# A batched matmul with x loaded ahead of its weights, all casts on VectorE, all PSUM copies on ScalarE, and one buffer of cast weights and of x_t

## The chip, the cores and the metric

The kernel runs on one core of a Trainium2 chip. The metric is the device time of one execution in microseconds (us), taken as the median of several executions. "Granted clock" is the TensorE clock that the profile records, as a share of full speed.

## The reference

```python
# x (8, 16, 256, 512) float32, weight (8, 16, 512, 384) float32
def reference(x, weight):
    return np.matmul(x, weight).astype(np.float32)      # 128 products of 256x512 by 512x384
```

## The kernel before

The 128 batches go in 32 groups of four. For each group the DMA loads x in one transfer (2.10 MB) and the weights in two (1.57 MB each), and the result leaves in one store (1.57 MB). The operands are cast to bf16, x is transposed by TensorE, and 128 matmuls of 128x384 make the result. Each engine has its own loop and waits on counting semaphores; `BIAS` is an offset that keeps the counts positive.

```python
    XS, WS, OS = 2, 2 * G // D, 4       # slots of x_sb, w_sb (half a group each), out_sb
    BS, TS, WBS = 1, 2, 2 * G           # buffers of x_bf, x_t, and of cast weights (per batch)
    PT, PO = 4, 2                       # PSUM buffers of transposes and of products
    LAG = 4                             # groups loaded ahead

    def load(e, t, U, s):               # SyncE: the two halves of w, then x
        n = t * U + s
        for d in range(G // D):
            ...
            e.wait_ge(w_cast, n * (G * S) + ((d + 1) * D * S - 2 * G * S))
            e.dma_start(w_sb[slot][:], ...).then_inc(w_in[slot], 16)
        ...
        e.wait_ge(x_cast, n * T + (1 - XS) * T)
        e.dma_start(x_sb[s % XS][:], ...).then_inc(x_in[s % XS], 16)

    def prepare(e, t, U, s):            # VectorE: casts of w, then copies of x_t
        n = t * U + s
        e.wait_ge(p_made, n * T + (BIAS - T))     # products of the group before last are done
        ...                                       # 8 casts of w_sb into w_bf
        for q in range(T):                        # T = 4
            e.wait_ge(t_made, n * T + (q + 1 + BIAS))
            e.tensor_copy(out=x_t[s % TS][:, 2 * q : 2 * q + 2], in_=pt[...][:].bitcast(bf16))

    def multiply(e, t, U, s):           # TensorE
        ...                             # 16 transposes (4 for each x_bf cast), then 128 matmuls
```

ScalarE casts x (`cast_x`) and copies the products out of PSUM (`copy_out`).

Of the kernel before, what the change touches and what calls it, by code (L numbers as in the profile page):

```python
# [9 lines left out]


@with_exitstack
def kernel(
# [6 lines left out]
    nc = tc.nc  # L20
    P = 128

    b1, b2, M, K = x.shape
# [4 lines left out]
    x_rows = x.rearrange("b1 b2 m k -> (b1 b2 m) k")  # L28
# [4 lines left out]
    bf16 = mybir.dt.bfloat16  # L33
# [6 lines left out]
    G = 4  # L40
    C = P // G
    R = G * M // P
    T = R // 2
# [3 lines left out]
    NG = B // G  # L47

    XS, WS, OS = 2, 2 * G // D, 4
    BS, TS, WBS = 1, 2, 2 * G  # L50
    PT, PO = 4, 2

    LAG = 4

    ctx.enter_context(tc.tile_critical(no_gpsimd_drain=True))  # L55

    def sbuf(name, shape, dtype, n):
        return [
            ctx.enter_context(nc.sbuf_tensor(f"{name}{s}", shape, dtype)) for s in range(n)
        ]  # L60

    def psum(name, shape, dtype, n):
        return [
            ctx.enter_context(nc.psum_tensor(f"{name}{s}", shape, dtype)) for s in range(n)
        ]

    def sems(name, n):
        return [tc.alloc_semaphore(f"{name}{s}") for s in range(n)]
# [3 lines left out]
    x_sb = sbuf("x_sb", [P, R, K], fp32, XS)  # L72

    x_bf = sbuf("x_bf", [P, R, S, HP, KO], bf16, BS)
    x_t = sbuf("x_t", [P, R, KO // 2, P, 2], bf16, TS)
# [3 lines left out]
    pt = psum("pt", [P, 2, KO // 2, P], fp32, PT)  # L79
# [5 lines left out]
    id_done, x_cast, w_cast, t_made, t_copied, p_made, o_copied = (  # L85
        sems(name, 1)[0]
        for name in (
            "id_done", "x_cast", "w_cast", "t_made", "t_copied", "p_made", "o_copied"
        )
    )  # L90
    x_in, w_in, o_out = sems("x_in", XS), sems("w_in", WS), sems("o_out", OS)


    BIAS = 8


    def load(e, t, U, s):
        n = t * U + s
        for d in range(G // D):
            slot = (s * (G // D) + d) % WS  # L100
            if not isinstance(n, int) or n >= 2:
                e.wait_ge(w_cast, n * (G * S) + ((d + 1) * D * S - 2 * G * S))
            e.dma_start(  # L103
                w_sb[slot][:],
                w_rows[bass.ds(n * (G * K) + d * (D * K), D * K)].rearrange(
                    "(p k) n -> p k n", k=S * KO
                ),
            ).then_inc(w_in[slot], 16)
        if not isinstance(n, int) or n >= XS:
            e.wait_ge(x_cast, n * T + (1 - XS) * T)  # L110
        e.dma_start(  # L111
            x_sb[s % XS][:],
            x_rows[bass.ds(n * (G * M), G * M)].rearrange("(p r) k -> p r k", r=R),
        ).then_inc(x_in[s % XS], 16)

    def store(e, t, U, s, pieces=1):
        n = t * U + s
        dram = o_rows[bass.ds(n * (G * M), G * M)].rearrange("(p r) n -> p r n", r=R)
        for q in range(pieces):
            rows = slice(q * R // pieces, (q + 1) * R // pieces)  # L120
            e.wait_ge(o_copied, n * T + ((q + 1) * T // pieces + BIAS))
            e.dma_start(out=dram[:, rows], in_=out_sb[s % OS][:, rows]).then_inc(
                o_out[s % OS], 16
            )

    def cast_x(e, t, U, s, q):
        n = t * U + s
        if q == 0:
            e.wait_ge(x_in[s % XS], (t * (U // XS) + s // XS) * 16 + 16)
        e.wait_ge(t_made, n * T + (q + 1 - T + BIAS))  # L130
        rows = slice(2 * q, 2 * q + 2)
        e.copy(  # L132
            out=x_bf[s % BS][:, rows],
            in_=x_sb[s % XS][:, rows].rearrange("p r (q s c) -> p r s q c", s=S, c=KO),
        ).then_inc(x_cast, 1)

    def prepare(e, t, U, s):
        n = t * U + s
        e.wait_ge(p_made, n * T + (BIAS - T))
        for d in range(G // D):  # L140
            slot = (s * (G // D) + d) % WS
            e.wait_ge(
                w_in[slot], (t * (U * G // D // WS) + s * G // D // WS) * 16 + 16
            )
            for a in range(D):
                for h in range(S):
                    e.tensor_copy(  # L147
                        out=w_bf[(s * G + d * D + a) % WBS][h * HP : (h + 1) * HP],
                        in_=w_sb[slot][a * HP : (a + 1) * HP, h * KO : (h + 1) * KO, :],
                    ).then_inc(w_cast, 1)  # L150
        for q in range(T):
            e.wait_ge(t_made, n * T + (q + 1 + BIAS))
            e.tensor_copy(  # L153
                out=x_t[s % TS][:, 2 * q : 2 * q + 2],
                in_=pt[(s * T + q) % PT][:].bitcast(bf16),
            ).then_inc(t_copied, 1)

    def multiply(e, t, U, s):
        n = t * U + s
        words = x_bf[s % BS][:].rearrange("p r s q c -> p r (s q c)").bitcast(fp32)  # L160
        for q in range(T):
            e.wait_ge(x_cast, n * T + (q + 1))
            e.wait_ge(t_copied, n * T + (q + 1 - PT + BIAS))
            for rr in range(2):
                for h in range(KO // 2):
                    ins = e.transpose(  # L166
                        pt[(s * T + q) % PT][:, rr, h, :],
                        words[:, 2 * q + rr, h :: KO // 2],
                        identity[:],
                    )  # L170
            ins.then_inc(t_made, 1)
        e.wait_ge(w_cast, n * (G * S) + G * S)
        for q in range(T):
            e.wait_ge(t_copied, n * T + (q + 1 + BIAS))
            e.wait_ge(o_copied, n * T + (q + 1 - PO + BIAS))
            for rr in range(2):
                for ko in range(KO):
                    for i in range(G):
                        mine = slice(i * C, (i + 1) * C)
                        ins = e.matmul(  # L180
                            po[(s * T + q) % PO][mine, rr, :N],
                            x_t[s % TS][:, 2 * q + rr, ko // 2, mine, ko % 2],
                            w_bf[(s * G + i) % WBS][:, ko, :],
                            start=(ko == 0),
                            stop=(ko == KO - 1),
                        )
            ins.then_inc(p_made, 1)

    def copy_out(e, t, U, s, q):
        n = t * U + s  # L190
        if q == 0:
            e.wait_ge(o_out[s % OS], (t * (U // OS) + s // OS) * 16 + 16)
        e.wait_ge(p_made, n * T + (q + 1 + BIAS))  # L193
        e.copy(  # L194
            out=out_sb[s % OS][:, 2 * q : 2 * q + 2, :],
            in_=po[(s * T + q) % PO][:, :, :N],
        ).then_inc(o_copied, 1)
# [7 lines left out]
    def on_sync(e):  # L205
        U = OS
        for n in range(LAG):
            load(e, 0, NG, n)
        rounds = (NG - LAG) // U
        with e.Fori(0, rounds) as t:  # L210
            for s in range(U):
                load(e, t, U, LAG + s)
                store(e, t, U, s)
        for n in range(rounds * U, NG):
            if n + LAG < NG:
                load(e, 0, NG, n + LAG)
            store(e, 0, NG, n, T if n == NG - 1 else 1)
        for s in range(OS):
            e.wait_ge(o_out[s], 16 + 16 * (NG // OS + (T - 1 if s == (NG - 1) % OS else 0)))

    def on_vector(e):
        U = 2
        e.sem_inc(t_copied, BIAS)
        with e.Fori(0, NG // U) as t:
            for s in range(U):
                prepare(e, t, U, s)

    def on_tensor(e):
        U = 2
        e.sem_inc(t_made, BIAS)  # L230
        e.sem_inc(p_made, BIAS)
        e.wait_ge(id_done, 2)

        pe = mybir.EngineType.PE
        with nc.Fori(0, NG // U, engines=OrderedEngineSet([pe]), head_slot={pe: 0}) as t:
            for s in range(U):
                multiply(e, t, U, s)

    def on_scalar(e):
        U = OS  # L240
        e.sem_inc(o_copied, BIAS)
        for s in range(OS):
            e.sem_inc(o_out[s], 16)

        with e.Fori(0, NG // U) as t:
            for s in range(U):
                for q in range(T):
                    cast_x(e, t, U, s, q)
                for q in range(T):
                    copy_out(e, t, U, s, q)  # L250

    on_gpsimd(nc.gpsimd)
    on_sync(nc.sync)
    on_vector(nc.vector)
    on_tensor(nc.tensor)
    on_scalar(nc.scalar)


# [28 lines left out]
```

## Time and profile before

| | before |
|---|---|
| time, median of 3 | 518.83 us (518.81 to 519.08) |
| span of the profiled execution | 517.2 us |
| mean granted clock | 0.803 |
| VectorE busy per group | 10.4 us |
| ScalarE busy per group | 7.4 us |
| DMA per group, at 429 GB/s | 15.9 us |

The prediction below shows the lines and the sums that these numbers come from. The profile is to be read in this order: the DMA row of the 40 slices (is the memory full?), the chain that ended last (what set the end?), and then the groups with what ended the idle time in front of them (which waits stand between the engines?). Here the DMA is full (90% or more in every slice but the first and the last) and the engines are not (VectorE 64%, TensorE 59%, ScalarE 46%).

### The profile page before, as it was taken

The numbers are of one execution on the slowest core, as the hardware profiler recorded it, in microseconds if no ns is written. First come the engines' busy times: TensorE is split into PE (matmuls) and PEld (weight loads), VectorE is DVE, ScalarE is ACT, GpSimd is POOL, SyncE is SP. The second block draws the span as 40 slices with busy tenths as digits, with TensorE's granted clock in tenths as the row PEclk, the third lists the DMA queues.
The fourth block names the chain that finished last, engine by engine and source line by source line (L and its number), as shares of the span: only waits on it lengthen the run. The fifth ranks groups of instructions, "written<-read, shape, count | busy, mean of one in ns | idle before, by whom it ended". The sixth has DMA issues, their size and how long they took to land.

```text
span 517.2 us, 11523 instructions
## 1 busy us (share of the span) xinstructions
PE 306.6 (59%) x4608; PEld 200.6 (39%) x4608; DVE 332.8 (64%) x384; ACT 236.7 (46%) x264; POOL 0.7 (0%) x6
## 2 busy tenths in 40 slices
PE   0478776556665457645577554776446765467752
PEld 0345444334443334433344332444324443244431
DVE  3698875667556676556675566855658656676550
ACT  0465564443644436435355354454444544544441
POOL 0000000000000000000000000000000000000000
PEclk9998877878777887878777778877788877778777
DMA  8999999999999999999999999999999999999996
GB/s 340 430 423 424 424 432 426 429 428 430 432 427 427 427 428 432 429 427 430 426 431 431 426 429 430 427 432 427 427 429 429 427 433 425 430 428 430 429 428 251
DMA packets 18869, 218.18 MB, mean 422 GB/s; under 512 B 2096, under 2 KB 2096, under 8 KB 2608
## 3 DMA queue, kind: packets, MB, share of 16 engines
q1 hardware_dynamic: 18864, 218.11, 99.3%
q8 instruction: 3, 0.05, 0.0%
q14 instruction: 2, 0.02, 0.0%
HBM read 167.77 MB, written 50.33 MB: 422 GB/s over the span
## 4 chain that ended last, share of the span: by engine, by line
DMA 81%; ACT 10%; PE 4%; issue 3%; ACTq 0%; SPq 0%
DMA x_sb<-in_x_dram 81%; ACT x_bf L132 9%; PE po L180 2%; PE pt L166 1%; ACTq L130 0%; ACT out_sb L194 0%; SPq L111 0%; SPq L103 0%; ACT L132 0%; ACTq L193 0%; SPq L282 0%; SPq L55 0%
## 5 line engine op out<-in xcount | busy, mean ns | idle before, releaser
L147 DVE CAST w_bf<-w_sb 64x1536 bf16<-64x1536 f32 x256 | 244.4, 955 | 47.2 <-DMA w_sb<-in_weight_dram 38.5
L166 PE MATMUL pt<-identity,x_bf 128*128 128x128 f32 x512 | 123.7, 425 | 199.3 <-ACT x_bf L132 199.1
L180 PE MATMUL po<-w_bf,x_t 128*32 128x384 bf16 x4096 | 185.1, 342 | 1.0 <-issue 1.0
L166 PEld LDWEIGHTS pt<-identity,x_bf 128*128 128x128 f32 x512 | 91.8, 216 | 232.1 <-issue 218.3
L194 ACT COPY out_sb<-po 128x768 f32<-128x768 f32 x128 | 102.2, 798 | 147.2 <-PE po L180 147.2
L153 DVE COPY x_t<-pt 128x1024 bf16<-128x1024 bf16 x128 | 88.4, 691 | 122.3 <-PE pt L166 121.8
L132 ACT CAST x_bf<-x_sb 128x1024 bf16<-128x1024 f32 x128 | 124.4, 1042 | 80.9 <-DMA x_sb<-in_x_dram 80.8
L180 PEld LDWEIGHTS po<-w_bf,x_t 128*32 128x32 bf16 x4096 | 108.8, 101 | 73.8 <-issue 14.2
L132 ACT ACT_TABLE_LOAD x8 | 10.3, 1283 | 42.9 <-DMA x_sb<-in_x_dram 42.9
masks.py:199 POOL TENSOR_SCALAR_AFFINE_SELECT identity<-identity 128x128 f32<-128x128 f32 x1 | 0.3, 292 | 0.2 <-POOL identity L200 0.2
L200 POOL MEMSET identity<- 128x128 f32 x1 | 0.2, 204 | 0.5 <-SPq L55 0.5
L271 POOL MEMSET const-bfloat16-1.0<- 128x1 bf16 x1 | 0.1, 101 | 0.0
L271 POOL MEMSET const-uint8-127<- 128x1 uint8 x1 | 0.1, 101 | 0.0
L271 POOL MEMSET const-float32-0.0<- 128x1 f32 x1 | 0.1, 98 | 0.2 <-issue 0.2
L271 POOL MEMSET const-float32-1.0<- 128x1 f32 x1 | 0.1, 98 | 0.0
## 6 DMA issues: line engine op xcount, KB each, us to landing
w_sb<-in_weight_dram SPq DMA_DIRECT2D x64, 1536.0 KB, 27.5
x_sb<-in_x_dram SPq DMA_DIRECT2D x32, 2048.0 KB, 27.5
out_dram<-out_sb SPq DMA_DIRECT2D x31, 1536.0 KB, 30.7
out_dram<-out_sb SPq DMA_DIRECT2D x4, 384.0 KB, 5.9
```

The costliest lines, as they stand in the source:

```text
L132: e.copy(out=x_bf[s % BS][:, rows], in_=x_sb[s % XS][:, rows].rearrange("p r (q s c) -> p r s q c", s=S, c=KO),).then_inc(x_cast, 1)
L147: e.tensor_copy(out=w_bf[(s * G + d * D + a) % WBS][h * HP : (h + 1) * HP], in_=w_sb[slot][a * HP : (a + 1) * HP, h * KO : (h + 1) * KO, : ...
L153: e.tensor_copy(out=x_t[s % TS][:, 2 * q : 2 * q + 2], in_=pt[(s * T + q) % PT][:].bitcast(bf16),).then_inc(t_copied, 1)
L166: ins = e.transpose(pt[(s * T + q) % PT][:, rr, h, :], words[:, 2 * q + rr, h :: KO // 2], identity[:],)
L180: ins = e.matmul(po[(s * T + q) % PO][mine, rr, :N], x_t[s % TS][:, 2 * q + rr, ko // 2, mine, ko % 2], w_bf[(s * G + i) % WBS][:, ko, :], ...
L194: e.copy(out=out_sb[s % OS][:, 2 * q : 2 * q + 2, :], in_=po[(s * T + q) % PO][:, :, :N],).then_inc(o_copied, 1)
L200: e.memset(identity[:], 0.0).then_inc(id_done, 1)
L271: nc = _bacc.Bacc("TRN2", target_bir_lowering=False, num_devices=1)
```

## The change

VectorE takes all casts (x, then w), ScalarE takes all copies out of PSUM (x_t, then products). The cast weights and x_t get one buffer in place of two, which saves memory in SBUF. x is loaded ahead of its weights because VectorE now casts x first. TensorE's loop covers one group in place of two, and three groups are loaded ahead in place of four.

```diff
-    BS, TS, WBS = 1, 2, 2 * G
+    BS, TS, WBS = 1, 1, G
-    LAG = 4
+    LAG = 3
     def load(e, t, U, s):
         n = t * U + s
+        (wait for x_cast, start the transfer of x)
         for d in range(G // D):
             (wait for w_cast, start the transfer of half a group of w)
-        (wait for x_cast, start the transfer of x)
     def cast_x(e, t, U, s, q):
-        e.copy(
+        e.tensor_copy(
-    def prepare(e, t, U, s):
-        e.wait_ge(p_made, n * T + (BIAS - T))
+    def cast_w(e, t, U, s):
+        e.wait_ge(p_made, n * T + BIAS)        # now: the products of the group just before
         ... (8 casts, as before)
-        for q in range(T):
-            (wait for t_made, copy x_t on VectorE)
+    def evacuate(e, t, U, s, q):               # on ScalarE
+        e.wait_ge(p_made, n * T + BIAS)
+        e.wait_ge(t_made, n * T + (q + 1 + BIAS))
+        e.copy(out=x_t[s % TS][:, 2 * q : 2 * q + 2], in_=pt[...][:].bitcast(bf16))
     def on_tensor(e):
-        with nc.Fori(0, NG // U, ...) as t:
-            for s in range(U):
-                multiply(e, t, U, s)
+        with e.Fori(0, NG) as t:
+            multiply(e, t, 1, 0)
```

The loops of VectorE and ScalarE are cut here to what they call: VectorE `cast_x` four times and then `cast_w`; ScalarE `evacuate` four times and then `copy_out` four times.

More of the change, by code (lines that the diff above doesn't have):

```diff
@@ L8 @@
 from concourse._compat import with_exitstack
-from concourse.ordered_engine_set import OrderedEngineSet
 @with_exitstack
@@ L98, in load @@
         n = t * U + s
+        if not isinstance(n, int) or n >= XS:
+            e.wait_ge(x_cast, n * T + (1 - XS) * T)
+        e.dma_start(
+            x_sb[s % XS][:],
+            x_rows[bass.ds(n * (G * M), G * M)].rearrange("(p r) k -> p r k", r=R),
+        ).then_inc(x_in[s % XS], 16)
         for d in range(G // D):
@@ L108, in load @@
             ).then_inc(w_in[slot], 16)
-        if not isinstance(n, int) or n >= XS:
-            e.wait_ge(x_cast, n * T + (1 - XS) * T)
-        e.dma_start(
-            x_sb[s % XS][:],
-            x_rows[bass.ds(n * (G * M), G * M)].rearrange("(p r) k -> p r k", r=R),
-        ).then_inc(x_in[s % XS], 16)
     def store(e, t, U, s, pieces=1):
@@ L150, in prepare @@
                     ).then_inc(w_cast, 1)
-        for q in range(T):
-            e.wait_ge(t_made, n * T + (q + 1 + BIAS))
-            e.tensor_copy(
-                out=x_t[s % TS][:, 2 * q : 2 * q + 2],
-                in_=pt[(s * T + q) % PT][:].bitcast(bf16),
-            ).then_inc(t_copied, 1)
+    def evacuate(e, t, U, s, q):
+        n = t * U + s
+        e.wait_ge(p_made, n * T + BIAS)
+        e.wait_ge(t_made, n * T + (q + 1 + BIAS))
+        e.copy(
+            out=x_t[s % TS][:, 2 * q : 2 * q + 2],
+            in_=pt[(s * T + q) % PT][:].bitcast(bf16),
+        ).then_inc(t_copied, 1)
     def multiply(e, t, U, s):
@@ L222, in on_vector @@
         U = 2
-        e.sem_inc(t_copied, BIAS)
         with e.Fori(0, NG // U) as t:
             for s in range(U):
-                prepare(e, t, U, s)
+                for q in range(T):
+                    cast_x(e, t, U, s, q)
+                cast_w(e, t, U, s)
     def on_tensor(e):
-        U = 2
         e.sem_inc(t_made, BIAS)
@@ L232, in on_tensor @@
         e.wait_ge(id_done, 2)
-        pe = mybir.EngineType.PE
-        with nc.Fori(0, NG // U, engines=OrderedEngineSet([pe]), head_slot={pe: 0}) as t:
-            for s in range(U):
-                multiply(e, t, U, s)
+        with e.Fori(0, NG) as t:
+            multiply(e, t, 1, 0)
     def on_scalar(e):
         U = OS
+        e.sem_inc(t_copied, BIAS)
         e.sem_inc(o_copied, BIAS)
@@ L247, in on_scalar @@
                 for q in range(T):
-                    cast_x(e, t, U, s, q)
+                    evacuate(e, t, U, s, q)
                 for q in range(T):
```

## The prediction

> **What bounds the kernel now.** I read the overview first, then the table of costliest groups, the chain that ended last, and the timeline with the table of stretches, for one pass and for the end.
>
> ```profile
> DMA  8999999999999999999999999999999999999996
> ...
> HBM read 167.77 MB, written 50.33 MB: 422 GB/s over the span
> ...
> DMA 81%; ACT 10%; PE 4%; issue 3%; ACTq 0%; SPq 0%
> ```
>
> The DMA engines are full in every slice but the first and last, and the chain is 81% transfer of x. The 40 slices show about 429 GB/s, so a group of four batches (6.82 MB: 5.24 loaded, 1.57 stored) takes 6.82/0.429 = 15.9 us, and there are 32 groups. This period is what any other limit has to beat.
>
> ```profile
> L147 DVE CAST w_bf<-w_sb 64x1536 bf16<-64x1536 f32 x256 | 244.4, 955 | 47.2 <-DMA w_sb<-in_weight_dram 38.5
> L166 PE MATMUL pt<-identity,x_bf 128*128 128x128 f32 x512 | 123.7, 425 | 199.3 <-ACT x_bf L132 199.1
> L180 PE MATMUL po<-w_bf,x_t 128*32 128x384 bf16 x4096 | 185.1, 342 | 1.0 <-issue 1.0
> L194 ACT COPY out_sb<-po 128x768 f32<-128x768 f32 x128 | 102.2, 798 | 147.2 <-PE po L180 147.2
> L153 DVE COPY x_t<-pt 128x1024 bf16<-128x1024 bf16 x128 | 88.4, 691 | 122.3 <-PE pt L166 121.8
> L132 ACT CAST x_bf<-x_sb 128x1024 bf16<-128x1024 f32 x128 | 124.4, 1042 | 80.9 <-DMA x_sb<-in_x_dram 80.8
> ```
>
> Per group VectorE works 8 x 0.955 + 4 x 0.691 = 10.4 us, ScalarE 4 x 1.042 + 4 x 0.798 = 7.4 us. No engine is near 15.9 us by its own work. So the change can hurt only by a chain of waits from group to group.
>
> ```profile
> 103.45 6.23 PE L180 MATMUL po<-w_bf,x_t 128*32 128x384 bf16 x128
> ...
> 105.72 7.86 DVE L147 CAST w_bf<-w_sb 64x1536 bf16<-64x1536 f32 x8 [1.46 <-DMA w_sb<-in_weight_dram]
> 105.84 0.80 ACT L194 COPY out_sb<-po 128x768 f32<-128x768 f32 x1 [3.56 <-PE po L180]
> ...
> 94.98:98.38 3.40, 0.00 (x0) 0.00 (x0) 2.56 (x3) 0.00 (x0) 0.00 (x0) 1.00 0.97 413
> 98.40:99.50 1.10, 0.00 (x0) 0.00 (x0) 0.00 (x0) 1.10 (x2) 0.00 (x0) 0.50 1.02 436
> ...
> 101.85:105.20 3.35, 3.35 (x32) 1.97 (x34) 1.89 (x3) 0.42 (x1) 0.00 (x0) 0.50 1.03 437
> 105.25:109.60 4.35, 4.35 (x108) 2.57 (x100) 3.79 (x4) 2.40 (x3) 0.00 (x0) 1.00 1.03 438
> ```
>
> The first two lines show that the eight weight casts of the next group (7.86 us back to back) run beside the products of this one: two sets of cast weights make that possible. The stretches (PE busy first, granted clock and DMA last) show the TensorE clock. After 3.4 us without work it falls to 0.50, and it returns to 1.00 only after a stretch filled with work. Through the whole trace the changes lie on a grid of 3.413 us. A slot with about 40% work or less ends in a fall, and one with 77% still gave no return. In the present kernel the transposes (3.7 to 4.0 us, just before the products) pay most of the warming up. At full clock the 128 products take 5.38 us, here 6.23.
>
> [...]
>
> **The change, part by part.**
> - *Casts of x to VectorE, copies of x_t to ScalarE.* [...] Off the path.
> - *One buffer of x_t.* The copies now wait for the products of the group before. From the end of those products: transposes some 2.8 us (four at full clock take 0.74)[...]. Less than the casts that run beside them; free.
> - *TensorE's loop over one group.* 32 returns in place of 16; what one costs falls where TensorE waits anyway. Up to some 2.5 us free.
> - *Three groups loaded ahead in place of four.* With two slots of x and four half-group slots of w, loads are bound by free slots anyway. A transfer now takes 27.5 us from issue to landing, so the queue is deep; the casts would have to fall behind by over 20 us to empty it. Free.
> - *One buffer of cast weights.* This is the one that matters. The casts of group n+1 cannot start before the last product of group n, which cannot start before the last cast of n. The ring: 7.86 (eight casts) + 0.13 (from a ScalarE cast's end to its transposes at 497.83; I take it for VectorE too) + 5.41 (from the first product at 501.51 to the engine that takes the last result, at 506.92) = 13.4 us at full clock. That would hide under 15.9.
>
> But TensorE now idles during the casts: 8.0 less 2.8 for transposes, about 4.3 to 5.2 us, right before the products. So the products start at half clock. Cold, four products take 0.32 us in place of 0.1625, so c us of cold work cost 0.5 c. By the grid, products that start s us into a slot stay cold until the next wholly filled slot ends: c = 6.83 - s, or 3.41 - s when they start within about 0.1 us of an edge. Now one turn after another by hand, where only what the ring is longer than 4 slots (13.65) moves s. From s = 0.05: c = 3.36, ring 13.4 + 1.7 = 15.1, so s = 1.5. There c = 5.3, ring 16.05, so s = 3.9, that is 0.5 in the next slot. There c = 6.3, ring 16.55, so s = 3.4, the edge again. The three turns last 14 slots, 47.8 us: a ring of **15.9 us** on average, with mean c 5.0. I chose this cycle because small errors of 13.4 (up to about 0.05) fall back into it. Other phases give mean c of 4.2 to 5.5, a ring of 15.5 to 16.2.
>
> **The sum.** The first x lands near 9.9 us, the weights at 13.6 and 17.3 (here the first three loads have landed by 17.37, the first by 8.7). Casts end at 21.4, and cold products at about 29.4. 31 turns of 15.9 end at 522. The tail: last copy 0.8, issue 0.5, [...]and some 3.5 us that the span now has after its last store: 7.7. Span 530; the time is 1.6 above the span (518.83 against 517.2): about 531.5.
>
> **Rivals.**
> - *The DMA stays the bound* (ring below 15.7): for it speak the full queue and the 2 us between 13.4 and 15.9 should the clock stay up; a slow return of TensorE's loop would even help, by shortening its idle time. The floor is then not 518.8: the last load is now a half of w, landing near 500.2 (today's last x at 496.55, plus one store of 3.7 that goes before it). Behind it come 3.93 of casts, 0.13, 5.41 + 2.3 and the 7.7: 519.6, with 1.6 about 521.
> - *The clock settles on the worst phases, or handovers cost more than I took*: ring 16.2 to 16.4, 29.4 + 31 x 16.3 + 9.3 = 544. For it: each wait now stands on the path, and 0.1 us in it costs 3 us.
> [...]
> - *Faster*: I see no way; the bytes at the present rate fill the time.
>
> I weigh the ring at 15.9 with the floor beside it and take 529.5 us, range 520.5 to 542. The line of 2% is at 529.2, so slower has 0.52, within 2% has 0.47, faster 0.01.
>
> **What would show it.** Right: weight casts starting with "PE po" as what ended their idle time, not the DMA; products of 7 to 8.5 us with a clock of 0.50 at their start; a spacing of weight casts of 15.9 us; DMA slices with digits under 9 or rates a few GB/s under 429. The DMA still at 9 throughout and a chain of x or w transfers would mean the first rival. [...] What would make all of it wrong: products that start warm, casts of w that are no longer 0.955 us beside ScalarE's PSUM reads, or transfers that starve because the queue is shallower than I took it.

The sum came to 531.5 us, and with the floor weighed in to 529.5. The tail of 7.7 us held 2.9 us for the landing of the last store, and it is also in the 521 us of the first rival. (After the result the page of the changed kernel has 2.6 us from issue to landing for stores of that size.)

What the prediction reads of the TensorE clock can be counted in the trace of the kernel before, by setting the clock record beside TensorE's recorded work in each slot of the grid. All changes lie within 1 ns of the grid. After each of the 22 slots without work the clock is 0.50. Of the cold slots with transposes alone, the 23 filled to 77% or less stay at 0.50 and the nine filled to 96% or more return to 1.00. Of the warm slots, those that end in a fall are filled to 44% or less, and no slot filled to less than 43% kept the clock.

## The result, and the profile after

| | before | after |
|---|---|---|
| time, median of 4 each | 518.92 us (518.81 to 519.08) | 520.54 us (520.23 to 520.97) |
| span of the profiled execution | 517.2 us | 518.7 us |
| mean granted clock | 0.803 | 0.812 |

The ratio is 1.0031, with a 95% interval of 1.0014 to 1.0049. The change costs 1.6 us, or 0.3%. The prediction had said 529.5 us, 2.1% slower. The measured time lies at the very edge of its range (520.5 to 542).

The overview of the changed kernel, with the chain that ended last:

```profile
DMA  8999999999999999999999999999999999999994
...
HBM read 167.77 MB, written 50.33 MB: 421 GB/s over the span
...
DMA 34%; DVE 31%; PE 29%; issue 5%; DVEq 0%; SPq 0%; ACT 0%
```

The slices are still full, but only a third of the chain is transfer, against 81% before. For about half of the run a ring sets the pace, that is, a closed chain of waits in which VectorE waits for TensorE and TensorE for VectorE; for the other half it is the DMA.

The groups of the changed kernel (busy us, mean ns of one, then idle time in front and what ended it):

```profile
L182 PE MATMUL po<-w_bf,x_t 128*32 128x384 bf16 x4096 | 234.6, 403 | 200.5 <-DVE w_bf L146 200.5
L146 DVE CAST w_bf<-w_sb 64x1536 bf16<-64x1536 f32 x256 | 244.4, 955 | 85.8 <-PE po L182 63.9
...
L131 DVE CAST x_bf<-x_sb 128x1024 bf16<-128x1024 f32 x128 | 80.0, 688 | 95.5 <-DMA x_sb<-in_x_dram 95.3
L155 ACT COPY x_t<-pt 128x1024 bf16<-128x1024 bf16 x128 | 120.5, 1033 | 8.1 <-PE pt L168 8.1
```

The first two lines are the ring: the products wait for the weight casts (200.5 us), and the weight casts wait for the products (63.9 us). Before, the products hardly waited (1.0 us) and the weight casts waited for the DMA. The other two lines are the swap: a cast of x on VectorE takes 688 ns (1042 on ScalarE), a copy of x_t on ScalarE 1033 ns (691 on VectorE).

The timeline of VectorE in the changed kernel, each line the eight weight casts of one group (start, duration, and in brackets the idle time in front with what ended it):

```profile
196.97 7.86 DVE L146 CAST w_bf<-w_sb 64x1536 bf16<-64x1536 f32 x8 [2.90 <-PE po L182]
211.77 7.86 DVE L146 CAST w_bf<-w_sb 64x1536 bf16<-64x1536 f32 x8 [1.72 <-PE po L182]
227.68 7.86 DVE L146 CAST w_bf<-w_sb 64x1536 bf16<-64x1536 f32 x8 [1.70 <-PE po L182]
243.05 7.86 DVE L146 CAST w_bf<-w_sb 64x1536 bf16<-64x1536 f32 x8 [1.15 <-DMA w_sb<-in_weight_dram]
...
275.19 7.86 DVE L146 CAST w_bf<-w_sb 64x1536 bf16<-64x1536 f32 x8 [1.42 <-PE po L182]
290.86 7.86 DVE L146 CAST w_bf<-w_sb 64x1536 bf16<-64x1536 f32 x8 [1.15 <-DMA w_sb<-in_weight_dram]
...
497.89 7.86 DVE L146 CAST w_bf<-w_sb 64x1536 bf16<-64x1536 f32 x8 [1.15 <-DMA w_sb<-in_weight_dram]
```

Two turns of the ring last 14.80 and 15.91 us, and these two alternate from the third group on: 30.71 us for two, so 15.36 us for one. That is 0.57 us less than the 15.93 us that the DMA takes for a group in the second half ((497.89 - 243.05) / 16). The first casts start at 12.57 us, while a run paced by the DMA from its start would have needed them at 497.89 - 31 x 15.93 = 4.1. The ring makes up these 8.5 us in fifteen turns, and from 243.05 us on the DMA bounds the kernel again. Even there the casts of every third group still wait for products, as at 275.19 us (16.20 us after the ones before), but the next ones make it up (15.67 us).

### The profile page after: what moved, and what is told of

Read it like the earlier page. It is cut to its first block, busy times and chain, and to the rows that moved or that the text cites. A ratio compares the mean times of both kernels' runs of the same rounds, so it can differ in the third digit from the quotient of the medians.

```text
span 518.7 us, 11458 instructions
## 1 busy us (share of the span) xinstructions
PE 303.8 (59%) x4608; PEld 205.9 (40%) x4608; DVE 324.4 (63%) x384; ACT 230.7 (44%) x264; POOL 0.7 (0%) x6
## 2 busy tenths in 40 slices
DMA packets 18867, 218.14 MB, mean 421 GB/s; under 512 B 2096, under 2 KB 2096, under 8 KB 2608
## 4 chain that ended last, share of the span: by engine, by line
DMA 34%; DVE 31%; PE 29%; issue 5%; DVEq 0%; SPq 0%; ACT 0%
DMA w_sb<-in_weight_dram 34%; DVE w_bf L146 31%; PE po L182 29%; DVEq L225 0%; ACT out_sb L196 0%; DVEq L129 0%; SPq L100 0%; SPq L108 0%; DVEq L141 0%; SPq L282 0%; SPq L54 0%
## 5 line engine op out<-in xcount | busy, mean ns | idle before, releaser
L182 PE MATMUL po<-w_bf,x_t 128*32 128x384 bf16 x4096 | 234.6, 403 | 200.5 <-DVE w_bf L146 200.5
L146 DVE CAST w_bf<-w_sb 64x1536 bf16<-64x1536 f32 x256 | 244.4, 955 | 85.8 <-PE po L182 63.9
L182 PEld LDWEIGHTS po<-w_bf,x_t 128*32 128x32 bf16 x4096 | 140.8, 117 | 288.1 <-issue 205.8
L131 DVE CAST x_bf<-x_sb 128x1024 bf16<-128x1024 f32 x128 | 80.0, 688 | 95.5 <-DMA x_sb<-in_x_dram 95.3
L155 ACT COPY x_t<-pt 128x1024 bf16<-128x1024 bf16 x128 | 120.5, 1033 | 8.1 <-PE pt L168 8.1
L168 PE MATMUL pt<-identity,x_bf 128*128 128x128 f32 x512 | 71.3, 293 | 9.8 <-DVE x_bf L131 9.8
L168 PEld LDWEIGHTS pt<-identity,x_bf 128*128 128x128 f32 x512 | 65.1, 209 | 19.6 <-issue 19.6
L155 ACT ACT_TABLE_LOAD x8 | 10.3, 1283 | 1.7 <-PEq L233 1.6
```

The costliest lines, as they stand in the source:

```text
L131: e.tensor_copy(out=x_bf[s % BS][:, rows], in_=x_sb[s % XS][:, rows].rearrange("p r (q s c) -> p r s q c", s=S, c=KO),).then_inc(x_cast, 1)
L146: e.tensor_copy(out=w_bf[(s * G + d * D + a) % WBS][h * HP : (h + 1) * HP], in_=w_sb[slot][a * HP : (a + 1) * HP, h * KO : (h + 1) * KO, : ...
L155: e.copy(out=x_t[s % TS][:, 2 * q : 2 * q + 2], in_=pt[(s * T + q) % PT][:].bitcast(bf16),).then_inc(t_copied, 1)
L168: ins = e.transpose(pt[(s * T + q) % PT][:, rr, h, :], words[:, 2 * q + rr, h :: KO // 2], identity[:],)
L182: ins = e.matmul(po[(s * T + q) % PO][mine, rr, :N], x_t[s % TS][:, 2 * q + rr, ko // 2, mine, ko % 2], w_bf[(s * G + i) % WBS][:, ko, :], ...
```

## Why the ring is 15.36 us and not 15.9

The arithmetic of a turn is eight casts, a handover, the products at full clock, and half of the time c that they run cold (in the two turns below, 2.64 and 4.90 us cold made the products 1.25 and 2.36 us longer than 5.41). The pieces as measured are 7.86 us, 0.24 us (casts end at 219.63, products start at 219.87) and 5.41 us: 13.51 + 0.5 c. Two turns, from the timeline of TensorE in the changed kernel:

```profile
205.06 6.66 PE L182 MATMUL po<-w_bf,x_t 128*32 128x384 bf16 x128 [6.03 <-DVE w_bf L146]
...
219.87 7.77 PE L182 MATMUL po<-w_bf,x_t 128*32 128x384 bf16 x128 [6.04 <-DVE w_bf L146]
```

The table of stretches shows the clock in the slots of the 3.413 us grid in which these products lie (in this trace, too, the clock changes within 1 ns of such a grid). The columns are the stretch and its length, busy time (and instructions) of TensorE, its weight loads, VectorE, ScalarE and GpSimd, then the granted clock, the DMA share and GB/s. The last two lines are of a turn of the second half, whose products start at 314.87 us.

```profile
204.29:207.68 3.39, 2.62 (x36) 1.52 (x40) 0.66 (x2) 0.00 (x0) 0.00 (x0) 0.50 1.00 424
207.70:211.10 3.40, 3.40 (x92) 2.38 (x88) 2.35 (x4) 2.24 (x3) 0.00 (x0) 1.00 1.01 426
...
217.95:221.34 3.39, 1.47 (x20) 0.88 (x24) 1.65 (x2) 0.00 (x0) 0.00 (x0) 0.50 1.01 433
221.36:224.75 3.39, 3.39 (x48) 1.92 (x44) 1.27 (x3) 0.80 (x1) 0.00 (x0) 0.50 1.00 423
224.77:228.16 3.39, 3.39 (x77) 2.34 (x69) 1.69 (x4) 2.08 (x3) 0.00 (x0) 1.00 1.02 431
...
313.52:316.91 3.39, 2.04 (x28) 1.26 (x32) 1.08 (x2) 0.00 (x0) 0.00 (x0) 0.50 0.97 416
316.93:320.33 3.40, 3.40 (x52) 1.91 (x44) 1.25 (x3) 0.90 (x2) 0.00 (x0) 0.50 1.02 433
```

A slot that was filled to 2.62 of 3.41 us (77%) with products brought the clock back at its end: the next slot is at 1.00. A slot filled to 1.47 us (43%) or 2.04 us (60%) did not, and the next, full slot still ran at 0.50. So products that start 0.8 us into a slot stay cold for only 2.6 us, where the prediction gave them 6.0.

The same can be counted over the whole trace, by setting the clock record beside TensorE's busy time in each cold slot. Of 51 cold slots with products alone in the changed kernel, the 19 filled to 61% or less did not bring the clock back and the 32 filled to 76% or more did. Of 32 with transposes alone in the kernel before, none up to 77% did and all from 96% on did.

With these readings the prediction's own arithmetic closes in two turns. From 0.8 us into a slot: c = 2.6, a turn of 14.8, which is 1.15 more than four slots, so the next products start 1.9 into a slot. There c = 6.83 - 1.9 = 4.9, a turn of 15.9, which is 2.3 more than four slots, so the next start is 4.2 or 0.8 us into the next slot. The two turns together are nine slots, 30.7 us, as measured. The mean c is 3.7 us, where the prediction had 5.0.

## The experiments

Each kernel was timed against the kernel before on the same chip in the same rounds, five rounds each unless told otherwise; the kernel before had medians of 518.41 to 518.72 us there. "Changed kernel" is the one under study.

### First call: what sets the end, and what the ring is worth

The first theory of the 1.6 us was the tail: since weights now arrive last, a group's whole work stands after the last transfer. Its rivals were the ring itself and a smaller load lead.

**Two sets of cast weights in the changed kernel**, so that its ring is open (`a_two_w`):

```diff
-    BS, TS, WBS = 1, 1, G
+    BS, TS, WBS = 1, 1, 2 * G
-        e.wait_ge(p_made, n * T + BIAS)            # in cast_w
+        e.wait_ge(p_made, n * T + (BIAS - T))
-        with e.Fori(0, NG) as t:
-            multiply(e, t, 1, 0)
+        with e.Fori(0, NG // 2) as t:
+            for s in range(2):
+                multiply(e, t, 2, s)
```

> The changed kernel with two sets of cast weights (and TensorE's loop over two groups, which they need); the casts wait for the products of two groups before. Theory of the end: the ring is gone, weight casts follow the transfers from the first groups on, but the last load, its casts and its cold products stay where they were: 520.2 to 520.8 us, no gain. Theory of the ring: back to 518.9 us.

Measured: 518.84 us, ratio 1.0001 (0.9988 to 1.0015). The weight casts wait for the DMA again:

```profile
L146 DVE CAST w_bf<-w_sb 64x1536 bf16<-64x1536 f32 x256 | 244.4, 954 | 44.0 <-DMA w_sb<-in_weight_dram 32.3
```

The time is that of the kernel before, although the weights still come last and all other parts of the change but TensorE's loop are in. The tail alone therefore doesn't explain the 1.6 us, and the theory fell.

**Four groups ahead in the changed kernel** (`a_lag4`): `LAG = 3` becomes `LAG = 4`.

> The changed kernel with four groups loaded ahead in place of three, nothing else. Theory of the end (the ring averages 15.4 us, under the 15.9 us of a group's transfers, and the whole 1.6 us is lost after the last load): one store of 1.57 MB no longer goes ahead of the last loads, so the last weights land 3.7 us earlier and the last products end near 510.4 in place of 514.1; the queue's own drain is then the bound and the time is 518.5 to 519.2 us, that of the kernel before. Theory of the ring (the single buffer of cast weights slows the middle): 520.5 us as before this edit. Theory of the start (x first): 520.5 us.

Measured: 520.61 us, ratio 1.0040 (1.0026 to 1.0054). The load lead is not the cause.

**Each transpose three times over in the changed kernel** (`a_warm`), so that TensorE idles less in front of its products:

```diff
-            for rr in range(2):
+            for again, rr in [(a, r) for a in range(3) for r in range(2)]:
                 for h in range(KO // 2):
```

> The changed kernel with each transpose done three times over into the same place, so that TensorE is busy 6.6 us of the 8.1 us of casts and keeps its clock. Ring at full clock 13.5 us; weight casts wait for the DMA after a few groups already, not from 243 us on; products 5.4 to 5.5 us. Theory of the end: the last products lose their 2.7 us of half clock, end near 511.4, and the time is 518.4 to 519.2 us. Theory of the ring: also near 518.9, so this run alone doesn't tell them apart; theory of the start: 520.5.

Measured: 520.34 us, ratio 1.0033 (1.0020 to 1.0047), mean granted clock 0.931. The products go from 403 to 365 ns, the wait of the weight casts is again for the DMA, and the chain is 76% DMA. The shorter ring, hidden by the DMA, gained nothing here (520.34 against 520.54 us). But the 1.6 us stay, so it isn't the ring's length that costs them either.

**Weights ahead of x in the changed kernel** (`a_wfirst`): the transfer of x goes back behind the loop over the halves of w.

> The changed kernel with each group's weights loaded ahead of its x, as the kernel before has it. Theory of the end: VectorE casts x ahead of the weights in its own order, so in the last group all of 2.5 us of x casts and 7.9 us of weight casts come after the last landing (near 501.5): products start near 512.2 and end near 520, span near 525, time 525 to 528 us. Theory of the start (x first costs the 1.6 us): 518.9 us. Theory of the ring: 520.5.

Measured: 536.26 us (534.03 to 539.68), ratio 1.0323 (1.0303 to 1.0342), far more than expected. The timeline of VectorE in that kernel:

```profile
203.63 2.50 DVE L131 CAST x_bf<-x_sb 128x1024 bf16<-128x1024 f32 x4 [6.04 <-DMA x_sb<-in_x_dram]
206.04 4.89 DVE L146 CAST w_bf<-w_sb 64x1536 bf16<-64x1536 f32 x5
```

VectorE's casts stand in the trace in the order of the program, x and then weights. It waits 6.04 us for x (to 203.63 us), and its weight casts then follow at 206.04 with no idle time in the trace, so the weights had landed by then. A turn takes 16.3 us (189.75 to 206.04 for the weight casts). The order alone doesn't say why x comes only every 16.3 us when the DMA needs 15.9 for a group. The recorded landings do. The trace records 16 landings for each transfer, its shares (more on them below). From the fifth to the 24th group the middle share of x lands every 15.88 us, but the last one only every 16.28 us (73.39 to 382.78 us), and the casts of x follow it every 16.28 us (73.67 to 382.91 us). One late share paces this kernel: it falls behind the middle one by 1.8 us at the fifth group and by 10.3 us at the last. So "x ahead of its weights" isn't a part that can be left out of the change: it belongs with VectorE casting x first.

### Second call: is the slot arithmetic right?

If a turn is 13.51 + 0.5 c, a small, known time added to the casts must move the ring in steps. k of a group's eight weight casts were made in two halves of 768 columns each (`a_split2`, `a_split4`, `a_split8` for k = 2, 4, 8):

```diff
                 for h in range(S):
-                    e.tensor_copy(out=w_bf[...], in_=w_sb[...]).then_inc(w_cast, 1)
+                    parts = 2 if (d * D + a) * S + h < k else 1
+                    for c in range(parts):
+                        ks = slice(c * KO // parts, (c + 1) * KO // parts)
+                        ins = e.tensor_copy(out=w_bf[..., ks], in_=w_sb[...][:, ks])
+                    ins.then_inc(w_cast, 1)
```

> Two of 8 casts in two halves[...]. Theory of clock slots: four turns in 19 slots, 16.2 us a turn, 535 to 540 us. Rival without slots: ring 15.7 to 15.8, still under the transfers' 15.9, 520.5 to 522 us.

> The changed kernel with 4 of a group's 8 weight casts done in two halves of 768 columns[...]. Theory of clock slots (a start counts as a filled slot when up to about a quarter of the slot is past, and cold work costs 0.5 us per us): each turn settles on exactly five slots of 3.413, 17.07 us, and the time is 29 + 31 x 17.07 + 6.4 = 564 us. Rival without slots (the mean loss of 1.9 us by cold clock stays what it is): ring 16.1, time 534 to 538. Rival that the ring never matters: 520.5 to 521.5.

> All 8 casts in two halves[...]. Theory of clock slots: again five slots a turn, 17.07 us, 564 us, the same as with half of the added cost. Rival without slots: ring 16.8 to 16.9, 556 to 560 us. Rival that the ring never matters: 521 us.

Measured, four runs each:

| halved casts | eight casts take | mean turn | time | ratio (95%) |
|---|---|---|---|---|
| 0 | 7.86 us | 15.36 us | 520.54 us | 1.0031 (1.0014 to 1.0049) |
| 2 | 8.00 | 15.79 (31 turns, 12.52 to 502.06 us) | 526.51 (525.04 to 527.90) | 1.0151 (1.0128 to 1.0175) |
| 4 | 8.14 | 15.93 (three turns are 47.79) | 528.71 (528.61 to 529.60) | 1.0198 (1.0183 to 1.0212) |
| 8 | 8.42 | 16.4 (five turns are 81.9) | 546.05 (544.71 to 546.51) | 1.0524 (1.0509 to 1.0539) |

A half takes 551 ns, so a halved cast should cost 2 x 551 - 955 = 147 ns. Back to back it costs 0.07 us. I had reckoned with more, an estimate that no trace shows and that is cut from the expectations. So the steps came out smaller than expected, and none of the three expected times, which rested on it, came (535 to 540, 564 and 564 us by the slots). TensorE in the kernel with four halved casts:

```profile
53.45 6.71 PE L186 MATMUL po<-w_bf,x_t 128*32 128x384 bf16 x128 [6.31 <-DVE w_bf L149]
68.59 7.66 PE L186 MATMUL po<-w_bf,x_t 128*32 128x384 bf16 x128 [6.31 <-DVE w_bf L149]
84.67 8.14 PE L186 MATMUL po<-w_bf,x_t 128*32 128x384 bf16 x128 [6.31 <-DVE w_bf L149]
```

These three durations return throughout, and their turns of 15.14, 16.08 and 16.57 us are 14 slots. The arithmetic gives the same cycle. With 13.79 + 0.5 c, products that start 0.8 us into a slot have c = 2.6; the next start at 2.3 with c = 4.5; the next at 1.3, where the slot can be filled only to 62% (65% in the trace), the clock doesn't come back, and c = 5.5; and the next again at 0.8. So 0.28 us more in the casts makes the ring 0.57 us longer, and it costs 8.2 us of time. A ring of 15.79 us costs time as well, although it is shorter than the DMA's 15.93: it makes up only about 0.14 us a turn, 4.3 of the 8.5 us, and its last casts start at 502.06 us in place of 497.89.

**x ahead of its weights and three groups ahead in the kernel before** (`b_xfirst_lag3`): the transfer of x moves in front of the loop over the halves of w, and `LAG` is 3.

> The kernel before (two sets of cast weights, ScalarE casts x) with only the two changes of the loads: x ahead of its weights, three groups ahead. Theory of the end: these two alone put the last half of w at the end of the loads, near 501.5, with 3.9 us of casts, x_t copies and cold products behind it: 519.8 to 521 us, most or all of the 1.6 us. Theory of the ring: 518.9 us, since there is no ring.

Measured, four runs: 520.51 us (519.96 to 521.86), ratio 1.0040 (1.0026 to 1.0054). With two sets of cast weights, all engines as before and no ring, this costs as much as the whole change.

### Third call: which part of the loads, or TensorE's loop

The changed kernel once more (`after_again`), TensorE's loop over two groups in the changed kernel and nothing else (`a_loop2`, the last five lines of the first diff above), and the two parts of `b_xfirst_lag3` alone in the kernel before (`b_xfirst`, `b_lag3`).

> The changed kernel itself once more, for a second trace. In the runs so far the trace shows the 16 shares of each transfer landing apart: in the changed kernel the last share of the last x and w transfers lands 4.0 us behind the middle one, in the kernel before 2.8 us, with two sets of cast weights 2.7 us. If that belongs to the kernel: 3.5 to 4.5 us here too and 520.2 to 520.9 us. If it is chance of a run: anything from 2 to 5 us, and times spread by over 1 us.

> The changed kernel with TensorE's loop over two groups in place of one and nothing else (one set of cast weights stays). The run with two sets had this loop as well and came back to 518.8 us. If the set is what brought it back: 520.5 us here. If the loop did: 518.9 us.

> The kernel before with x ahead of its weights, four groups ahead as it has them. One store fewer goes ahead of the last load than in the run with three groups ahead, so casts and products of the last group end some 3.7 us earlier, behind which the store queue still drains: 518.5 to 519.2 us if the end is all there is to it; 520 us or more if x ahead itself makes the slowest share of the transfers fall behind.

> The kernel before with three groups loaded ahead in place of four, weights ahead of x. The last x lands 3.7 us later, near 500.3; casts, transposes, products and copies that now end at 507.7 then end near 511.4, and the last store lands near 514.3, still not behind the drain of the queue that ends the kernel at 515.8 now: 518.6 to 519.3 us.

| kernel | time | ratio (95%) |
|---|---|---|
| changed kernel again | 520.38 us | 1.0036 (1.0022 to 1.0050) |
| changed, TensorE's loop over two groups | 520.32 | 1.0032 (1.0018 to 1.0045) |
| before, x ahead of its weights | 520.33 | 1.0033 (1.0019 to 1.0047) |
| before, three groups ahead | 518.69 | 0.9999 (0.9986 to 1.0013) |

TensorE's loop and the load lead cost nothing. x ahead of its weights costs the kernel before 1.8 us, but it cost nothing in the changed kernel with two sets of weights. The parts don't add up, so something common to the slow ones was to be found.

### What the slow kernels share: one late share of every transfer

The trace records 16 landings for each transfer; I call them its shares. In the traces of the kernel before and of the changed kernel, VectorE and ScalarE waited 58 and 38 times for a transfer, and each time they started 0.02 to 0.14 us after a sixteenth landing. At the last load fifteen of the landings lie within 2.56 us in the kernel before and within 2.39 us in the changed one. The sixteenth falls behind over the run: it is 1.8 us behind the middle at 201 us and 2.8 at 488 us in the kernel before, 1.7 at 38 us, 3.2 at 199 us and 4.0 at 486 us in the changed one. From the ninth load on it never gains back more than 0.08 us from one load to the next in either trace. (The records don't name the shares; that the late one is the same all through is inferred from its steady distance.) I call its distance from the middle share at the last load its lag; the middle is the mean of the eighth and ninth. It is worked out from the recorded landings of one profiled execution of each kernel:

| kernel | lag, us | time, us |
|---|---|---|
| before, three groups ahead | 2.06 | 518.69 |
| changed, two sets of cast weights | 2.72 | 518.84 |
| before | 2.79 | 518.92 |
| changed, transposes three times | 3.97 | 520.34 |
| before, x ahead of its weights | 3.96 | 520.33 |
| changed kernel again | 4.02 | 520.38 |
| changed kernel | 4.04 | 520.54 |
| changed, TensorE's loop over two groups | 4.29 | 520.32 |
| changed, four groups ahead | 4.62 | 520.61 |
| before, x ahead and three groups ahead | 4.60 | 520.51 |

None of these lies between 2.8 and 3.9. The middle share of the last load keeps its time: with four groups ahead it lands at 493.76 us in the kernel before and at 493.98 with x ahead; with three groups ahead at 497.42 in the changed kernel and at 497.63 in that with two sets of weights. The memory as a whole is not slower in these; one share of sixteen is. The kernels that wait for a ring or for x up to the end stand outside this table, since their times follow from their turns: 6.97 us (`a_split2`), 10.20 (`a_split4`), 1.94 (`a_split8`), 10.28 (`a_wfirst`), and 2.69 (`b_one_w`, told below). TensorE does the same products in all of them, so the amount of its work alone doesn't set the lag. That the lag makes the time was still a correlation.

### Fourth call: TensorE's work as the cause of the lag

The kernels differ in when TensorE works while transfers run. So TensorE was given more work in the kernel before (`b_warm`, the edit of `a_warm`), and a quarter of its products in the kernel before with x ahead (`b_xfirst_quarter`) and in the changed kernel (`a_quarter`). The last two give a wrong result.

```diff
-                for ko in range(KO):
+                for ko in range(1):
-                            stop=(ko == KO - 1),
+                            stop=True,
```

> The kernel before with each transpose done three times over: TensorE works some 13 us of each 15.9 in place of 9.5. If TensorE's work beside the stores makes the slowest share of the transfers fall behind: a lag of 4 us or more at the last x and 520 to 521 us. If it has no part in it: lag 2 to 3 us and 518.5 to 519.2 us (the last products end some 4 us later, near 511, which the run with three groups ahead showed to be free).

> A wrong result on purpose. The kernel before with x ahead of its weights (520.3 us, lag 4.0), but only a quarter of the products (one of four 128-row pieces of k). If TensorE's work makes the lag: lag under 2.8 us and 518.5 to 518.9 us. If not: 520.2 us or more.

> A wrong result on purpose. The changed kernel with only a quarter of the products: the turn falls to some 10 to 11 us, so weight casts wait for the DMA from the second or third group on, and the last products end some 5 us earlier. If TensorE's work makes the lag: lag under 2.8 us, 518.5 to 518.9 us. If x ahead of its weights makes it whatever TensorE does: lag 4 us, 520.3 us.

| kernel | lag, us | time, us | ratio (95%) |
|---|---|---|---|
| before, transposes three times | 3.91 | 520.67 | 1.0038 (1.0024 to 1.0052) |
| before, x ahead, a quarter of the products | 2.18 | 517.97 | 0.9987 (0.9973 to 1.0001) |
| changed, a quarter of the products | 2.43 | 518.40 | 0.9992 (0.9978 to 1.0006) |

More TensorE work made the fast kernel slow (518.63 to 520.67 us), less made the slow ones fast (520.33 to 517.97 and 520.54 to 518.40), and the lag went along (2.79 to 3.91, 3.96 to 2.18 and 4.04 to 2.43). In all these edits the number of TensorE's instructions changes along with its busy time; the runs don't tell the two apart. And these kernels also have more or less work at their very end, which could do the same without any lag.

**One set of cast weights in the kernel before**, all else as it was (`b_one_w`): `WBS` is `G`, and `prepare` waits for `p_made, n * T + BIAS`.

> The kernel before with one set of cast weights and nothing else: ScalarE still casts x, VectorE still copies x_t, and does so behind the casts of w. The turn then has one x_t copy more: 7.86 + 0.24 + 0.69 + 0.2 + 5.41 = 14.4 us at full clock. By the slots of the clock (a start counts as filled with up to about a quarter of the slot past) each turn settles on five slots, 17.07 us: 29 + 31 x 17.07 + 6 = 560 to 566 us. Without slots (2 us of cold clock a turn): 16.4 us, 540 to 545 us. If one set cost nothing by itself: 518.7 us.

Measured: 539.11 us (four runs), ratio 1.0387 (1.0371 to 1.0403), less than either expectation. From its timeline, VectorE and TensorE:

```profile
182.38 2.48 DVE L153 COPY x_t<-pt 128x1024 bf16<-128x1024 bf16 x4
...
183.12 8.16 PE L180 MATMUL po<-w_bf,x_t 128*32 128x384 bf16 x128 [2.91 <-DVE x_t L153]
```

The products start 0.74 us into the four copies: they wait for the first copy of x_t only. From casts to products it is 8.63 us (174.49 to 183.12), against 8.10 in the changed kernel (211.77 to 219.87). With these 0.53 us more the mean turn is 16.17 us ((498.83 - 29.83) / 29) and the time 539, between `a_split4` and `a_split8`. So the single buffer alone costs 20 us in the kernel before. In the changed kernel it costs at most the 1.7 us between 520.54 and the 518.84 of `a_two_w`: the copies of x_t have left the ring for ScalarE, and the ring stays under the DMA's 15.93 us.

### Fifth call: the same work at the end, another history

To separate the lag from the work at the end, only the first 24 of the 32 groups were altered. `b_warm24` is the kernel before with each transpose three times there; `b_xfirst_quarter24` is the kernel before with x ahead and a quarter of the products there (wrong). The last eight groups are those of the kernel they start from. The diff is abridged: `multiply` also gets one argument more.

```diff
-        with nc.Fori(0, NG // U, ...) as t:
+        with nc.Fori(0, 12, ...) as t:
+            for s in range(U):
+                multiply(e, t, U, s, 3)        # transposes three times; or: one ko of four
+        with nc.Fori(12, 16, ...) as t:
             for s in range(U):
                 multiply(e, t, U, s)
```

> The kernel before, with each transpose three times over in the first 24 of the 32 groups only; the last eight groups, and so all the work that can stand at the end, are those of the kernel before. If TensorE's work makes one of the 16 shares of the transfers fall behind, and the end waits for that share, the lag of some 3 us that the kernel with extra transposes throughout had built up by 390 us stays to the end: lag of the last load about 3.4 to 3.9 us, time 519.7 to 520.4 us. If the longer work of the last groups was what made that kernel slower, the time is that of the kernel before, 518.4 to 518.9 us, whatever the lag.

> Wrong result on purpose. The kernel before with x ahead of its weights, and a quarter of the products in the first 24 groups only; the last eight groups have all their products, so the end has the same work as in the kernel with x ahead of its weights alone (520.33 us). If the lag of one share sets the end, it starts the last eight groups at about 2.2 us in place of 3.2 and grows by some 0.7 there: about 2.9 at the last load, time 518.9 to 519.5 us. If the work at the end sets the time, 520.2 to 520.6 us.

Measured: `b_warm24` 520.28 us, ratio 1.0036 (1.0023 to 1.0050), lag 3.87 us. `b_xfirst_quarter24` 518.89 us, ratio 1.0007 (0.9993 to 1.0020), lag 3.05 us. Both are where the lag puts them (a lag of 3.4 to 3.9 and of about 2.9 was expected), and neither is where its work at the end would (518.4 to 518.9 and 520.2 to 520.6).

The stretches at the end of the kernel before:

```profile
512.00:514.00 2.00, 0.00 (x0) 0.00 (x0) 0.00 (x0) 0.00 (x0) 0.00 (x0) 0.50 0.22 88
514.00:516.00 2.00, 0.00 (x0) 0.00 (x0) 0.00 (x0) 0.00 (x0) 0.00 (x0) 0.50 0.04 17
```

and of the kernel with more transposes in its first 24 groups:

```profile
512.00:514.00 2.00, 0.00 (x0) 0.00 (x0) 0.00 (x0) 0.00 (x0) 0.00 (x0) 0.50 0.31 126
514.00:516.00 2.00, 0.00 (x0) 0.00 (x0) 0.00 (x0) 0.00 (x0) 0.00 (x0) 0.50 0.06 26
516.00:518.00 2.00, 0.00 (x0) 0.00 (x0) 0.00 (x0) 0.00 (x0) 0.00 (x0) 0.50 0.02 8
```

All engines are done in both. The DMA share is a mean over 16 engines, so 0.06 is one of them (0.0625): the end waits for one share. It lands at 515.77 us in the first kernel and at 517.03 us in the second, 1.26 us later. The late share of the last whole store lands at 512.05 us in the first, 3.71 us after the middle share, and at 513.34 us in the second, 4.80 us after it. Its parts of the four small stores behind it then take 3.7 us in both. So 1.09 of the 1.26 us are lag (at the last load it was 3.87 - 2.79 = 1.08).

In the changed kernel the same lag takes another way to the end:

```profile
505.99 8.06 PE L182 MATMUL po<-w_bf,x_t 128*32 128x384 bf16 x128 [6.30 <-DVE w_bf L146]
...
514.10 0.80 ACT L196 COPY out_sb<-po 128x768 f32<-128x768 f32 x1 [0.50 <-PE po L182]
```

Its last weight casts start at 497.89 us, when the late share of that half of w has landed (497.80). With two sets of weights and a lag of 2.73 they start at 496.77. The products follow 1.13 us later (505.99 against 504.86), and the last store lands at 517.23 against 515.78. Their cold start (8.06 us, against 7.74) adds the rest. In the repeat the last casts waited for products (498.10 us), the products behind them were shorter (6.71 us), and there the end waited for the late share again, with a time of 520.38 us. So in the changed kernel the tail and the late share end within about 1 us of each other.

No version that beats both kernels came out of this. The bytes at the present rate fill the time (218.14 MB at 429 GB/s are 508 of the 518.7 us), and no variant with a right result was faster than the kernel before beyond scatter.

## Why the prediction was right or wrong

**The swap of the engines: right.** The cast of x took 688 ns on VectorE, the copy of x_t 1033 ns on ScalarE, and the weight casts stayed at 955. None of it is on the path.

**x_t, TensorE's loop, and the load lead: right.** `a_loop2`, `b_lag3` and `a_lag4` measured nothing beyond scatter for the loop and the lead. The single buffer of x_t was not tried by itself, but `a_two_w` has it and takes the time of the kernel before.

**The ring exists: right.** The weight casts wait for "PE po", products start cold and take 6.7 to 8.1 us. These are two of the signs that the prediction asked for. The other two, a spacing of 15.9 us and weaker DMA slices, didn't come.

**The ring's length: wrong, and this is the step that failed.** The step reads: "A slot with about 40% work or less ends in a fall, and one with 77% still gave no return", and from it, "products that start s us into a slot stay cold until the next wholly filled slot ends: c = 6.83 - s, or 3.41 - s when they start within about 0.1 us of an edge". The 77% had been read off transposes. With products a slot filled to 77% did bring the clock back. A start 0.8 us into a slot, where the prediction allowed about 0.1, thus still gave the early return, and the cycle settles there. The mean c is 3.7 us and not 5.0, and the ring is 15.36 us and not 15.9. The handover was mis-sized the other way, 0.24 us for 0.13. The prediction chose its cycle because errors of up to about 0.05 us fall back into it; the handover alone was off by twice that. Why transposes and products differ here no run shows.

**What the ring's length makes of the time: right.** With a ring of 15.93 us, which `a_split4` has, the time is 528.71 us; the sum of the prediction gave 531.5 for 15.9 (its 529.5 already weighs in the floor), too much mostly by its tail.

**The first rival was the true one, with a wrong reason for its size.** "The DMA stays the bound" came with 521 us, close to 520.54. It puts the tail of computing behind weights that land last. The trace does have that tail, but `a_two_w` has it too, at 518.84 us. Two errors in it nearly cancel, so that its 521 is so near is partly luck: the products end 2.1 us later than its sum has them (514.05 us; the last half of w lands at 501.46 in place of 500.2), and from there to the end of the span it takes 4.65 us (514.05 to 518.7) in place of 7.7. What costs the 1.6 us is a late share of the transfers, which the prediction didn't have at all. It showed in the profile before: the slice from 514 to 516 us at a DMA share of 0.04 with no engine at work.

**What stays open.** The runs show that TensorE's work in earlier groups raised the lag in the kernel before (2.79 to 3.87 us with more transposes in 24 groups; with x ahead, 3.05 to 3.96 us from a quarter of the products there to all), and that there the lag sets the end (1.09 of the 1.26 us). For the changed kernel it rests on its traces and on `a_quarter`, whose end is shorter too. They don't show how work in TensorE slows one share of a transfer, nor why the changed kernel with two sets of weights, which has the same TensorE work at other times, keeps a lag of 2.72 us. What a single buffer does to the lag is therefore known from these kernels only, and can't be worked out for others.

## What to carry to other kernels

Here one buffer of cast weights in place of two cost at most 1.7 us in the changed kernel, where the ring of waits that it closed took 15.36 us against the 15.93 of the DMA, and 20 us in the kernel before, where it took 16.17. With a ring of 15.79 us, still under the DMA's, the time was 526.51 us. So work out the length of such a ring before a buffer is dropped, and here that had to be to a few tenths of a microsecond, because the granted clock went back from 0.50 to 1.00 in some slots of the grid and not in others: 0.28 us of extra casts cost 8 us. Before a reading from one kind of instruction is used for another (a slot filled to 77% with transposes stayed cold, one with products did not), look for the other kind in the trace, and work out the neighbouring cycles as well, not only the one that the estimate falls on. When the memory is full all through and the time still moves by a microsecond or two, look at the last stretches for a DMA share of one engine, and compare the pace of the last landing with that of the middle one: in `a_wfirst` they differed by 0.4 us a group, and the kernel took 17.5 us longer.
